# Turned hidden activations in a SwiGLU feed-forward: their splits later in the written order, their transfers on one queue, and four down columns in three passes

## The chip, the cores and the metric

The kernel runs on one core of a Trainium2 chip. A core has a matmul engine (PE, with its weight loads shown as PEld), a vector engine (DVE), a scalar engine (ACT), a general engine (POOL, or GpSimd) and a queue engine (SP). Each takes its own instructions in order; DMA transfers are issued from the queues of SP, ACT and POOL. The metric is the device time of one execution, in microseconds (us); lower is better.

## The reference, cut to what matters

Two layers of a decoder trunk on 256 tokens of width 1024, all in float32. Each layer is a feed-forward, a token mixer, a cross-attention to a memory of 256 rows, and a second feed-forward:

```python
def swiglu(x, w_gate, w_up, w_down):
    return (jax.nn.silu(x @ w_gate) * (x @ w_up)) @ w_down

for l in range(DEPTH):                       # DEPTH = 2, D_MODEL = 1024, D_FF = 2816
    x = x + 0.5 * swiglu(rmsnorm(x, ffn1_norm[l]), ffn1_w_gate[l], ffn1_w_up[l], ffn1_w_down[l])
    h = rmsnorm(x, mix_norm[l])
    x = x + (even_mixer(h, ...) if l % 2 == 0 else odd_mixer(h, ...))
    x = x + memory_cross_attention(rmsnorm(x, xa_norm[l]), mem_n, ...)
    x = x + 0.5 * swiglu(rmsnorm(x, ffn2_norm[l]), ffn2_w_gate[l], ffn2_w_up[l], ffn2_w_down[l])
return rmsnorm(x, final_norm)
```

The four feed-forwards, in order of time: ffn1 of layer 0 (called the first here), ffn2 of layer 0 (the second), ffn1 of layer 1 (the third) and ffn2 of layer 1 (the last, after which only the final norm follows).

## The kernel before, in words

**Numbers in two halves.** Every float32 operand of a matmul is split into a high part (a copy rounded to fp32r) and a low part (the rest), and a product is made of three: high by high, high by low, low by high. A split is one ACT copy and one DVE subtraction. Weights are split so on the chip, in blocks of eight 128x128 tiles: lines 127 (ACT, `whi`) and 128 (DVE, `wlo`). There are five buffers of such blocks, and `Stream.take` asks for the block that is needed and four more ahead. The raw weights come from HBM in the order in which the program takes them, 16 tiles to a transfer, on SP's queue (line 102).

**The order of the work.** `Order.run` writes the program in an order of its own: it has a list of fillers (pieces of matmul work, each with a test that says from when it is ready, the piece, and its cost) and a heap of tasks that are due some time after something else (`pe.after(delay, fn, cost)`). Its clock advances by the costs, which are in ns of matmul time. A task is run between two fillers, at the first point at which it is due. The instructions written so are then put in order on each engine by a scheduler with a simulated timeline, which may let an instruction go ahead of an earlier one that it takes to be not ready. `tc.keep_in_program_order` pins an instruction behind the one written just before it on its engine.

**A feed-forward.** The hidden width of 2816 is 22 tiles of 128 (`FT`). `hidden(f0)` makes four of them: eight pieces of 2600 in the order's time, first the gate (line 554 applies silu, on ACT) and then the up product (line 558 multiplies, on DVE). The last two tiles, f0=20, have gate and up side by side in one group of four pieces (lines 565 and 566). In the first feed-forward the scale of the norm is known only after the first group. These matmuls (lines 533 to 535) keep the activations in place and stream 512 weight columns, so the result has tokens on partitions.

**The turn.** The down product needs h with its own index on partitions. `turned_back` does that: DVE transposes within 32x32 blocks (line 507) into a tile `t` (named v or k2 in turn, one buffer each; v and k in the profile), one DMA writes it to a DRAM tile named turn (line 510), and four DMAs read it back with the blocks moved (line 512). Groups of four tiles use POOL's queue, the last group of two uses ACT's. Then each of the tiles is split: ACT copy in line 518, DVE subtraction in line 519. These are written directly after the transfers.

**The down columns.** `downs` makes the eight output tiles j, each a sum over 22 tiles k of h (lines 393 and 394; the last column uses a narrower form, line 398 to 400). Columns 0 and 1 first take k = 0 to 19, then both take k = 20 and 21; the others take all 22 in one go. A column's sum is in an `acc` bank; there are four `acc` banks, two `sc` (score) banks and two `tr` banks. At a column's end line 585 adds it to x in two steps on DVE, and lines 318 and 319 (ACT and DVE) make the next norm's operand, with squares for the norm's sum (lines 329, 333). The last feed-forward uses `down_tok` instead, which keeps tokens on partitions and takes two tiles of h at a time.

The next function bodies are those that the change touches, with the profile's line numbers.

Of the kernel before, what the change touches and what calls it, by code (L numbers as in the profile page):

```python
# [15 lines left out]
F32 = mybir.dt.float32  # L16
F32R = mybir.dt.float32r
AF = mybir.ActivationFunctionType
ALU = mybir.AluOpType
# [6 lines left out]
KT = D // P  # L26
S = 256
FF = 2816
FT = FF // P
# [189 lines left out]
def paired(t):  # L219

    return t.rearrange("p (b a) -> p a b", b=2)


def halves(t):

    return t.rearrange("p (b a) -> p b a", b=2)


def unpaired(ps):

    return ps.rearrange("p (a b) -> p b a", b=2)
# [12 lines left out]
def build(nc, tc, ctx, a):  # L244
# [6 lines left out]
    def acc_tile():  # L251
        return psum.tile([P, 512], F32, name="acc", bufs=4)
# [10 lines left out]
    def w2():  # L263
        return act.tile([P, 512], F32, name="w2", bufs=6)
# [5 lines left out]
    x = consts.tile([P, KT, S], F32, name="x")  # L270
# [22 lines left out]
    pe = Order()  # L293
# [176 lines left out]
    def h_tile():  # L470
        return Split(act.tile([P, 2 * S], F32R, name="h", bufs=FT))
# [26 lines left out]
    def ffn(which, layer, n, nxt, first=False, last=False):  # L498
        h = [None] * FT
        gate, up = f"{which}_w_gate", f"{which}_w_up"  # L500

        def turned_back(f0, s, c):

            t = act.tile([P, 8 * c * 32], F32, name=("v", "k2")[f0 // 4 % 2], bufs=1)
            to = t.rearrange("p (b u c i) -> p u c b i", b=4, u=2, c=c)
            for u in range(2):
                nc.vector.transpose(to[:, u], s[u].rearrange("p (c b j) -> p c b j", c=c, b=4))
            queue = nc.gpsimd if c == 4 else nc.scalar
            d = dram.tile([P, 8 * c * 32], F32, name="turn", bufs=2)
            queue.dma_start(d, t)  # L510
            for b in range(4):
                queue.dma_start(t[32 * b:32 * b + 32].rearrange("j (a x) -> j a x", a=4),
                                d.rearrange("(a j) (b x) -> b j a x", a=4, b=4)[b])
            back = t.rearrange("p (a u c i) -> p c u a i", a=4, u=2, c=c)
            for i in range(c):
                h[f0 + i] = x2 = h_tile()
                hi, lo = (m.rearrange("p u (a i) -> p u a i", a=4) for m in (x2.hi, x2.lo))
                nc.scalar.activation(hi, back[:, i], AF.Copy)
                nc.vector.tensor_tensor(lo, back[:, i], hi.bitcast(F32), op=ALU.subtract)  # L519

        def rows_of(name, c, bank, evac, other=None):

            ps = []

            def part(ks):
                def go():
                    if ks[0] == 0:
                        ps.extend(bank() for _ in range(2))
                    for k in ks:
                        wh, wl = (paired(w) for w in ws.take(name, layer, k * P, c, 4, other=other))  # L530
                        for u in range(2):
                            xh, xl = (n.x[k].v[:, u, m] for m in range(2))
                            nc.tensor.matmul(ps[u], xh, wh, start=k == 0, stop=False)  # L533
                            nc.tensor.matmul(ps[u], xh, wl, start=False, stop=False)  # L534
                            nc.tensor.matmul(ps[u], xl, wh, start=False, stop=k == KT - 1)  # L535
                    ws.flush()
                    if ks[-1] == KT - 1:
                        when_scaled(n, lambda: evac(ps))

                return always, go, len(ks) * 1300  # L540

            return [part(range(k, k + 2)) for k in range(0, KT, 2)]

        def hidden(f0):
# [24 lines left out]
            if f0 + 4 > FT:  # L569
                return rows_of(gate, f0 * P, acc_tile, both, up)  # L570
            return (rows_of(gate, f0 * P, sc_tile if f0 // 4 % 2 else acc_tile, gated) +
                    rows_of(up, f0 * P, acc_tile, product))

        def down(j, ks, cell):
            def go():
                if ks[0] == 0:
                    cell.append(acc_tile())
                ps = cell[0]
                ws.fine = j == KT - 1
                for k in ks:  # L580
                    w = ws.take(f"{which}_w_down", layer, k * P, j * P)
                    (mm_narrow if ws.fine else mm)(ps, w, h[k], k == 0, k == FT - 1)
                if ks[-1] == FT - 1:
                    for part in (ps[:, :S],) if ws.fine else (ps[:, :S], ps[:, S:]):
                        nc.vector.scalar_tensor_tensor(halves(x[:, j]), unpaired(part), 0.5, halves(x[:, j]),
                                                       op0=ALU.mult, op1=ALU.add)
                    normed_tile(nxt, j, x[:, j], x)
                ws.flush()

            return always, go, len(ks) * 327  # L590

        def downs():

            cells = [[] for _ in range(KT)]
            early = range(FT // 4 * 4)
            late = range(FT // 4 * 4, FT)
            return ([down(j, early, cells[j]) for j in range(2)] + [down(j, late, cells[j]) for j in range(2)] +
                    [down(j, range(FT), cells[j]) for j in range(2, KT)])

        def down_tok():  # L600

            late = 2 * (ws.BUFS - 1)
            pss, got, mean = {}, {}, [EPS, EPS]

            def part(fs, *regions):

                c = regions[0][1] // 512

                def go():
                    for f in fs:
                        if (f, c) not in got:
                            got[f, c] = ws.take(f"{which}_w_down", layer, f * P, c * 512, 4)
                        for reg in regions:
                            u, c0, c1 = reg
                            if f == 0:
                                pss[reg] = (sc_tile if c == 1 and c1 - c0 == 512 else acc_tile)()[:, :c1 - c0]
                            ps = pss[reg]
                            wh, wl = (paired(w)[:, (c0 - c * 512) // 2:(c1 - c * 512) // 2] for w in got[f, c])  # L620
                            hh, hl = (h[f].v[:, u, m] for m in range(2))
                            nc.tensor.matmul(ps, hh, wh, start=f == 0, stop=False)
                            nc.tensor.matmul(ps, hh, wl, start=False, stop=False)  # L623
                            nc.tensor.matmul(ps, hl, wh, start=False, stop=f == FT - 1)  # L624
                    if fs[-1] == FT - 1:
                        for u, c0, c1 in regions:
                            evac_tok(u, slice(c0, c1), pss[u, c0, c1])

                return always, go, sum(len(fs) * (c1 - c0) * 654 // 512 for _, c0, c1 in regions)

            def evac_tok(u, at, ps):
                y = xtok[:, u, at]
                nc.vector.scalar_tensor_tensor(y, ps, 0.5, y, op0=ALU.mult, op1=ALU.add)
                ms = act.tile([P, 1], F32, name="mean", bufs=4)
                junk = w2()[:, :at.stop - at.start]
                nc.vector.tensor_tensor_reduce(junk, y, y, 1.0 / D, mean[u], ALU.mult, ALU.add, ms)
                mean[u] = ms
                if at.stop < D:
                    nc.gpsimd.tensor_tensor(y, y, gfin[:, at], op=ALU.mult)
                    return  # L640
                r = act.tile([P, 1], F32, name="rcol", bufs=2)
                nc.gpsimd.tensor_tensor(r, ms, mhalf[:, 0:1], op=ALU.pow)
                nc.vector.tensor_tensor(y, y, gfin[:, at], op=ALU.mult)
                out = a["out"][u * P:(u + 1) * P]
                cuts = (0, 384, 704, D)
                nc.scalar.activation(xtok[:, u, :cuts[1]], xtok[:, u, :cuts[1]], AF.Copy, scale=r)
                nc.scalar.dma_start(out[:, :cuts[1]], xtok[:, u, :cuts[1]])
                for i, j in zip(cuts[1:], cuts[2:]):
                    nc.vector.tensor_scalar(xtok[:, u, i:j], xtok[:, u, i:j], r, None, op0=ALU.mult)
                    nc.sync.dma_start(out[:, i:j], xtok[:, u, i:j])  # L650

            end = range(FT - late, FT)
            right = ((0, 512, D), (1, 512, 768), (1, 768, D))
            return [part(range(i, i + 2), (0, 0, 512), (1, 0, 512)) for i in range(0, FT, 2)] + [
                part(range(FT - late), *right)] + [part(end, reg) for reg in right]

        if first:
# [469 lines left out]
    for k in range(KT):  # L1127
# [3 lines left out]
        cuts = (0, 1, SIDE) if k == 0 else (0, SIDE)  # L1131
# [9 lines left out]
    early = {}  # L1141
# [115 lines left out]
```

## Time and profile before

| what | value |
|---|---|
| three timed runs | 972.92, 975.81 (median), 977.94 us |
| the profiled execution, whole | 979.09 us |
| its span, first to last instruction | 977.3 us |
| PE busy in the span | 957.3 us (98%) |
| ACT, DVE, POOL busy | 556.4, 683.2, 106.8 us |
| mean granted clock of PE | 0.992 |

A row of the order of time has its start, its length, the engine, the line and operation, output<-input, how many were merged, and in brackets how long the engine stood idle before it and what ended that. A queue of an engine (ACTq, POOLq) shows what it issues. A row of the groups has the busy time, the mean of one in ns, and the idle time before the group with what ended most of it. A row of the waits has the total in us, the number, and the longest.

### The profile page before, as it was taken

The page shows a single profiled execution, that of the slowest core. Times are in us where ns is not written, and L with a number is a line of the kernel's source. Part 1 is how long each engine was busy: PE and PEld are TensorE (multiplying, and loading weights), DVE is VectorE, ACT ScalarE, POOL GpSimd, SP SyncE. Part 2 cuts the span into 40 slices and gives each one's busy share as a digit, 9 for nine tenths or more (in the row PEclk, how much of TensorE's full clock was granted, in tenths as well). Part 3 has the DMA queues.
Part 4 walks back from the last instruction along what each step waited for, and adds up shares of the span by engine and source line. Part 5 has one row for each costly group of instructions (what it writes and reads, how often), then busy time and mean ns, then how long its engine had stood idle before and what let it go on. Part 6 is the DMA issues. An engine that isn't in the chain of part 4 may idle for free.

```text
span 977.3 us, 15067 instructions
## 1 busy us (share of the span) xinstructions
PE 957.3 (98%) x5830; PEld 877.2 (90%) x5830; DVE 683.2 (70%) x1077; ACT 556.4 (57%) x903; POOL 106.8 (11%) x195
## 2 busy tenths in 40 slices
PE   9999969999999999999999999999999999999997
PEld 7888859999999988888998888999999998888896
DVE  7666557698878866666666666677887697677663
ACT  7554535498657754554555554555796585465541
POOL 0421110001000011120001111000000005511110
PEclk9999979999999999999999999999999999999999
DMA  9898765654444687866557787765635248987831
GB/s 372 317 369 278 251 214 203 216 215 148 165 165 136 243 273 259 266 236 206 211 207 234 249 258 260 227 222 190 243 130 195 93 173 291 322 274 233 267 137 43
DMA packets 39511, 219.67 MB, mean 225 GB/s; under 512 B 5768, under 2 KB 8840, under 8 KB 16784
## 3 DMA queue, kind: packets, MB, share of 16 engines
q1 hardware_dynamic: 27072, 187.44, 54.4%
q0 software_dynamic: 8912, 28.35, 9.7%
q10 hardware_dynamic: 3456, 2.93, 1.0%
q8 instruction: 45, 0.74, 0.3%
q14 instruction: 26, 0.21, 0.1%
HBM read 205.04 MB, written 16.80 MB: 227 GB/s over the span
## 4 chain that ended last, share of the span: by engine, by line
PE 86%; DMA 8%; issue 2%; POOL 2%; ACT 1%; DVE 1%; POOLq 0%; SPq 0%; DVEq 0%; ACTq 0%
PE acc L533 10%; PE acc L534 10%; PE acc L535 10%; PE acc L393 10%; PE acc L398 7%; PE acc L400 7%; PE acc L399 7%; PE acc L394 5%; DMA v<-turn 3%; PE sc L535 2%; PE sc L534 2%; PE sc L533 2%; DMA turn<-k 2%; PE acc L623 1%; PE acc L624 1%
## 5 line engine op out<-in xcount | busy, mean ns | idle before, releaser
L128 DVE TENSOR_TENSOR wlo<-raw,whi 128x1024 fp32r<-128x1024 f32 (+2 forms) x377 | 426.0, 1139 | 197.0 <-ACT whi L127 194.7
L127 ACT ACTIVATE whi<-raw 128x1024 fp32r<-128x1024 f32 (+2 forms) x377 | 367.0, 984 | 287.9 <-PE acc L535 121.1
L534 PE MATMUL acc<-wlo,x 128*128 128x512 f32 x576 | 218.5, 379 | 0.8 <-DVE wlo L128 0.8
L535 PE MATMUL acc<-whi,x 128*128 128x512 f32 x576 | 218.1, 379 | 0.0
L533 PE MATMUL acc<-whi,x 128*128 128x512 f32 x576 | 215.5, 380 | 1.4 <-ACT whi L127 1.4
L393 PE MATMUL acc<-h,whi 128*128 128x512 f32 x462 | 156.0, 390 | 9.9 <-DVE h L519 9.9
L394 PE MATMUL acc<-h,wlo 128*128 128x256 f32 x462 | 127.5, 277 | 0.0
L533 PEld LDWEIGHTS acc<-whi,x 128*128 128x128 f32 x576 | 108.8, 189 | 17.1 <-ACT whi L127 1.9
L534 PEld LDWEIGHTS acc<-wlo,x 128*128 128x128 f32 x576 | 108.9, 189 | 16.6 <-DVE wlo L128 1.4
L535 PEld LDWEIGHTS acc<-whi,x 128*128 128x128 f32 x576 | 108.9, 189 | 15.3
L393 PEld LDWEIGHTS acc<-h,whi 128*128 128x128 f32 x462 | 89.2, 194 | 23.5 <-DVE h L519 10.5
L394 PEld LDWEIGHTS acc<-h,wlo 128*128 128x128 f32 x462 | 90.7, 196 | 0.2
L400 PE MATMUL acc<-h,wlo 128*128 128x256 f32 x322 | 87.7, 275 | 0.0
L399 PE MATMUL acc<-h,whi 128*128 128x256 f32 x322 | 87.7, 275 | 0.0
L398 PE MATMUL acc<-h,whi 128*128 128x256 f32 x322 | 86.5, 277 | 0.0
L400 PE MATMUL acc<-x,wlo 128*128 128x256 f32 x304 | 84.1, 278 | 0.0
L399 PE MATMUL acc<-x,whi 128*128 128x256 f32 x304 | 83.8, 277 | 0.0
L398 PE MATMUL acc<-x,whi 128*128 128x256 f32 x304 | 83.3, 278 | 0.0
L399 PEld LDWEIGHTS acc<-h,whi 128*128 128x128 f32 x322 | 61.7, 192 | 0.1
L400 PEld LDWEIGHTS acc<-h,wlo 128*128 128x128 f32 x322 | 61.7, 192 | 0.1
L398 PEld LDWEIGHTS acc<-h,whi 128*128 128x128 f32 x322 | 60.6, 192 | 0.4 <-DVE x L461 0.2
L399 PEld LDWEIGHTS acc<-x,whi 128*128 128x128 f32 x304 | 58.2, 192 | 0.2
(220 smaller groups left out, 1402.8 us busy)
## 6 DMA issues: line engine op xcount, KB each, us to landing
raw<-in_w SPq DMA_DIRECT2D x171, 1024.0 KB, 5.0
turn<-v POOLq DMA_DIRECT2D x12, 512.0 KB, 3.3
v<-turn POOLq DMA_DIRECT2D x48, 128.0 KB, 4.6
turn<-k POOLq DMA_DIRECT2D x8, 512.0 KB, 4.6
k<-turn POOLq DMA_DIRECT2D x32, 128.0 KB, 5.4
dists<-line POOLq DMA_DIRECT2D x2, 1536.0 KB, 14.2
raw<-in_memT SPq DMA_DIRECT2D x3, 1024.0 KB, 5.0
raw<-in_w SPq DMA_DIRECT2D x6, 384.0 KB, 6.0
```

The lines of the kernel that those rows point to most:

```text
L127: for ins in (self.nc.scalar.activation(hi[:, at], src, AF.Copy), self.nc.vector.tensor_tensor(lo[:, at], src, hi[:, at].bitcast(F32), op= ...
L128: self.nc.vector.tensor_tensor(lo[:, at], src, hi[:, at].bitcast(F32), op=ALU.subtract)):
L393: nc.tensor.matmul(ps, w[0], x2.both, start=start, stop=False)
L394: nc.tensor.matmul(ps[:, :S], w[1], x2.high, start=False, stop=stop)
L398: nc.tensor.matmul(ps[:, :S], w[0], x2.high, start=start, stop=False)
L399: nc.tensor.matmul(ps[:, :S], w[0], x2.low, start=False, stop=False)
L400: nc.tensor.matmul(ps[:, :S], w[1], x2.high, start=False, stop=stop)
L533: nc.tensor.matmul(ps[u], xh, wh, start=k == 0, stop=False)
L534: nc.tensor.matmul(ps[u], xh, wl, start=False, stop=False)
L535: nc.tensor.matmul(ps[u], xl, wh, start=False, stop=k == KT - 1)
L623: nc.tensor.matmul(ps, hh, wl, start=False, stop=False)
L624: nc.tensor.matmul(ps, hl, wh, start=False, stop=f == FT - 1)
```

## The change

The split of the turned tiles becomes a function `split` that the order puts in 22000 (ns of its time) after the transfers were written, and its instructions are pinned in program order. All transfers of the turn go to GpSimd's queue, the last group's too. The down columns 0 to 3 are made in three passes over k, 0 to 15, 16 to 19 and 20 to 21; columns 4 to 7 take all 22 at once, and columns 4 and 5 take their banks from `sc`. A filler of the down product now tests whether the tiles of h that it names have been written (`have`), where it was always ready.

```diff
-            queue = nc.gpsimd if c == 4 else nc.scalar
             d = dram.tile([P, 8 * c * 32], F32, name="turn", bufs=2)
-            queue.dma_start(d, t)
+            nc.gpsimd.dma_start(d, t)
             for b in range(4):
-                queue.dma_start(t[32 * b:32 * b + 32].rearrange("j (a x) -> j a x", a=4),
-                                d.rearrange("(a j) (b x) -> b j a x", a=4, b=4)[b])
+                nc.gpsimd.dma_start(t[32 * b:32 * b + 32].rearrange("j (a x) -> j a x", a=4),
+                                   d.rearrange("(a j) (b x) -> b j a x", a=4, b=4)[b])
             back = t.rearrange("p (a u c i) -> p c u a i", a=4, u=2, c=c)
-            for i in range(c):
-                h[f0 + i] = x2 = h_tile()
-                hi, lo = (m.rearrange("p u (a i) -> p u a i", a=4) for m in (x2.hi, x2.lo))
-                nc.scalar.activation(hi, back[:, i], AF.Copy)
-                nc.vector.tensor_tensor(lo, back[:, i], hi.bitcast(F32), op=ALU.subtract)
+
+            def split():
+                for i in range(c):
+                    h[f0 + i] = x2 = h_tile()
+                    hi, lo = (m.rearrange("p u (a i) -> p u a i", a=4) for m in (x2.hi, x2.lo))
+                    tc.keep_in_program_order(nc.scalar.activation(hi, back[:, i], AF.Copy))
+                    tc.keep_in_program_order(nc.vector.tensor_tensor(lo, back[:, i], hi.bitcast(F32), op=ALU.subtract))
+
+            pe.after(22000, split, 0)
...
+        def have(ks):
+            return lambda: math.inf if any(h[k] is None for k in ks) else 0.0
+
         def down(j, ks, cell):
             def go():
                 if ks[0] == 0:
-                    cell.append(acc_tile())
+                    cell.append((sc_tile if j in (4, 5) else acc_tile)())
...
-            return always, go, len(ks) * 327
+            return have(ks), go, len(ks) * 327
 
         def downs():
 
             cells = [[] for _ in range(KT)]
-            early = range(FT // 4 * 4)
-            late = range(FT // 4 * 4, FT)
-            return ([down(j, early, cells[j]) for j in range(2)] + [down(j, late, cells[j]) for j in range(2)] +
-                    [down(j, range(FT), cells[j]) for j in range(2, KT)])
+            cuts = (0, FT // 4 * 4 - 4, FT // 4 * 4, FT)
+            return ([down(j, range(*cut), cells[j]) for cut in zip(cuts, cuts[1:]) for j in range(4)] +
+                    [down(j, range(FT), cells[j]) for j in range(4, KT)])
...
-                return always, go, sum(len(fs) * (c1 - c0) * 654 // 512 for _, c0, c1 in regions)
+                return have(fs), go, sum(len(fs) * (c1 - c0) * 654 // 512 for _, c0, c1 in regions)
```

The second `have` is in `down_tok`.

## The prediction

> **What bounds the kernel now.** I read the page first, then the waits of the matmul engine, then the order of time around each wait, engine by engine.
>
> ```profile
> span 977.3 us, 15067 instructions
> PE 957.3 (98%) x5830; PEld 877.2 (90%) x5830; DVE 683.2 (70%) x1077; ACT 556.4 (57%) x903; POOL 106.8 (11%) x195
> PE   9999969999999999999999999999999999999997
> PEclk9999979999999999999999999999999999999999
> ```
>
> PE is busy for 957.3 of 977.3 us, so no change of order can win more than the 20.0 us of idle time plus whatever the busy time contains of slow matmuls. The sixth slice (122 to 147 us) is the only inner one with a hole, and the same slice has the low clock. The wait of PE for a turned h (total, times, longest):
>
> ```profile
> PE acc L393 <- DVE h L519: 9.9, 2, 8.1
> ```
>
> Both are of a down column (L393) for the split of a turned h (L519). In order of time on PE, with a third and short wait for a weight split:
>
> ```profile
> 117.38 0.48 PE L534 MATMUL acc<-wlo,x 128*128 128x512 f32 x1 [0.78 <-DVE wlo L128]
> 122.45 0.38 PE L393 MATMUL acc<-h,whi 128*128 128x512 f32 x1
> 139.23 0.79 PE L393 MATMUL acc<-h,whi 128*128 128x512 f32 x1 [8.11 <-DVE h L519]
> 145.11 0.38 PE L393 MATMUL acc<-h,whi 128*128 128x512 f32 x1
> ...
> 437.33 0.38 PE L393 MATMUL acc<-h,whi 128*128 128x512 f32 x1
> 437.66 0.38 PE L393 MATMUL acc<-h,whi 128*128 128x512 f32 x1
> 447.84 0.48 PE L393 MATMUL acc<-h,whi 128*128 128x512 f32 x1 [1.83 <-DVE h L519]
> 449.03 0.63 PE L393 MATMUL acc<-h,whi 128*128 128x512 f32 x1
> 452.23 0.40 PE L393 MATMUL acc<-h,whi 128*128 128x512 f32 x1
> ```
>
> That is 10.7 us of waits; the other 9.3 us of idle time are the start and the tail, which the change does not touch. After a wait the matmuls run slow. A window of 5 us inside the first such stretch (busy time of PE, PEld, DVE, ACT and POOL, then the granted clock, the DMA share and GB/s):
>
> ```profile
> 140.00:145.00 5.00, 5.00 (x18) 4.26 (x17) 3.34 (x6) 3.67 (x5) 0.00 (x0) 0.50 0.14 38
> ```
>
> From 139.23 to 145.11 (5.88 us) PE ran at clock 0.50, which costs 2.9 us; from 449.03 to 452.23 (3.2 us) again, 1.6 us. So a wait costs itself and a slow stretch: 8.11 + 2.9 and 1.83 + 1.6, and 0.78 with nothing behind it.
>
> *A rule against the row:* the Trainium skill (TensorE: Matmul & The Clock Gate, What's actually happening) lets the clock fall only after an idle window of about 3.4 us. Here 1.83 us of idle were followed by a half clock. By the rule a left-over wait below 3.4 us would cost itself alone; by the row it costs 1.6 us more, and the row is what I use.
>
> **Why h came late.** ACT, DVE and the queues in the first feed-forward:
>
> ```profile
> 113.79 1.34 ACT L518 ACTIVATE h<-k 128x256 fp32r<-128x256 f32 x4 [9.65 <-DMA k<-turn]
> 114.24 1.43 DVE L519 TENSOR_TENSOR h<-k,h 128x256 fp32r<-128x256 f32 x4 [8.84 <-ACT h L518]
> 118.46 1.40 DVE L558 SCALAR_TENSOR_TENSOR w<-acc,rcol,w 128x512 f32<-128x512 f32 x2
> 122.50 0.59 POOL L510 DMA_DIRECT2D turn<-v  x1 [16.43 <-DVE v L507]
> 126.34 2.20 POOL L512 DMA_DIRECT2D v<-turn  x4 [3.24 <-DMA turn<-v]
> 127.34 0.34 ACTq L510 DMA_DIRECT2D turn<-k  x1
> 138.31 0.42 ACT L518 ACTIVATE h<-v 128x256 fp32r<-128x256 f32 x1 [9.47 <-DMA v<-turn]
> 138.42 0.34 ACTq L512 DMA_DIRECT2D k<-turn  x1
> 142.95 0.71 ACT L518 ACTIVATE h<-k 128x256 fp32r<-128x256 f32 x2
> ```
>
> The reader should see a chain of two links. ACT stood 9.65 us at the split of f0=12 for its transfer; DVE, in order too, stood 8.84 us behind it and came to the product of f0=16 (L558) only at 118.46, so the write of f0=16 went out at 122.50. Its data came back at 138.31, 15.8 us later, and the down column, begun at 122.45, needed it after 16 of its steps. And f0=20's reads, on ACT's own queue, could not go out before 138.42, behind that same split.
>
> **The change, part by part.** Write T for the moment when the last row matmul of a group is in. One down step (row to row, 437.33 to 437.66) is 0.33 us; the order's cost for it is 327, so its units are ns. Group f0=20 is 8 k of 1300, 10.4 us: T16 = 122.45 - 10.4 = 112.0 and T12 = 91.2 in the first feed-forward; T16 = 426.9 and T20 = 437.3 in the second.
>
> *Splits 22000 later.* A group of four is 20.8 us, so the split is put in after the next group's product and one further row part: T + 22 to T + 23.4. For f0=12 that is 113, and its data came at 113.79: ACT stands about 1 us, not 9.65, and the product of f0=16 is now ahead of that split on DVE. That takes the 0.78 us wait and the first link. In the second feed-forward, with DVE not held, the write of f0=16 goes out at:
>
> ```profile
> 432.71 0.56 POOL L510 DMA_DIRECT2D turn<-v  x1 [14.45 <-DVE v L507]
> 439.24 0.34 ACTq L510 DMA_DIRECT2D turn<-k  x1
> 446.91 0.42 ACT L518 ACTIVATE h<-v 128x256 fp32r<-128x256 f32 x1 [5.75 <-DMA v<-turn]
> ...
> 615.00 0.34 ACTq L510 DMA_DIRECT2D turn<-k  x1
> 621.51 2.29 ACTq L512 DMA_DIRECT2D k<-turn  x4
> 627.51 0.72 ACT L518 ACTIVATE h<-k 128x256 fp32r<-128x256 f32 x2 [1.60 <-DMA k<-turn]
> ```
>
> that is T16 + 5.8, and its data is there by T16 + 20.0. The first feed-forward then issues at 117.8 and, at its own slower 15.8 us, has the data at 133.6, T16 + 21.6.
>
> *Four columns in three passes.* Pass 1 is 4 x 16 steps, 20.9 us; pass 2 needs f0=16 at T20 + 20.9 = T16 + 31.3; pass 3 needs f0=20 at T20 + 26.2. The split of f0=16 is put behind the third column of pass 1 (T16 + 26.1 in the order; its instructions reach ACT at about T16 + 24.5, as weight splits run four blocks ahead), that of f0=20 behind the first column of pass 2 (T20 + 22.2). Both are past the data and ahead of the need. The passes alone would do it: even at today's times h of f0=16 (139.2) is before 122.45 + 20.9 = 143.4 and that of f0=20 (about 145) before 148.6. So 8.11 + 2.9 and 1.83 + 1.6 go.
>
> *All transfers on GpSimd's queue.* Five issues per feed-forward move, in all four. On ACT they lay beside the matmuls and win nothing themselves. On POOL they stand behind f0=16's four reads (126.34 + 2.20), which are out before f0=20's write (127.34); then a wait for the write and four issues at 0.55 us. From write to last data took 12.5 us at 615.00 to 627.51 on ACT's queue. Bounds in the first feed-forward: 127.34 + 12.5 = 139.8, early by 7 us; or with the longest rows, 11.1 us (127.34 to 138.42) for the write and 12.0 us (126.34 to 138.31) for the reads, 150.4: with 1.2 us of splits, 3 us after 148.6, and 1.6 to 2.9 us of half clock. So 0 to 6 us; I take 0, since the long rows both contain ACT's stand.
>
> *Against the change* the Trainium skill (SBUF — State Buffer, section SBUF: two separate sides) says that a DMA issued from GpSimd can be held while DVE has the port they share. This view of one line (min/median/max ns) shows no such hold:
>
> ```profile
> L512 POOL DMA_DIRECT2D v<-turn x48: 553/553/581, 40.7 to 911.6; - x48
> ```
>
> The 48 issues lie beside DVE at 70% busy and none took over 581 ns. By the rule each of the five issues could be held for one weight split of 1.23 us, and the far bound above would be 12 us in place of 6; by the row it stays at 6, and so I leave it.
>
> *Banks and the end of the columns.* Columns 0 to 3 keep all four acc banks until pass 3, columns 4 and 5 take the two score banks, free since the gate of f0=12. Column 2 needs the bank of f0=20's rows at T20 + 10.5; these were read before the turn of 127.34, T20 + 4.9. In pass 3 four columns end within 2.6 us where two did:
>
> ```profile
> L128 DVE TENSOR_TENSOR wlo<-raw,whi 128x1024 fp32r<-128x1024 f32 x316 | 385.5, 1227 | 188.0 <-ACT whi L127 186.5
> L319 DVE SCALAR_TENSOR_TENSOR x<-x,vecs 128x256 fp32r<-128x256 f32 x56 | 26.1, 478 | 1.2 <-ACT x L318 1.2
> L585 DVE SCALAR_TENSOR_TENSOR x<-acc,x 128x256 f32<-128x256 f32 x45 | 18.7, 422 | 9.3 <-PE acc L394 6.5 <-PE acc L400 2.3
> ```
>
> DVE gets 4 x (2 x 0.422 + 0.478) = 5.3 us at once. The weight splits' lead, four blocks of 8 steps or 10.5 us, hides it; without that lead it would be 5.3 us in each of three feed-forwards. Matmuls, weight bytes and vector work are the same in number. The test for a missing h acts in the order's time alone and puts no wait on the chip.
>
> *The pins.* Behind a split that stands on ACT queue the weight splits, and behind these PE. The place to watch is f0=4 of the first feed-forward, whose data comes latest after its group:
>
> ```profile
> 68.96 1.06 ACT L127 ACTIVATE whi<-raw 128x1024 fp32r<-128x1024 f32 x1 [1.53 <-PE acc L535]
> 82.96 1.33 ACT L518 ACTIVATE h<-k 128x256 fp32r<-128x256 f32 x4 [7.70 <-DMA k<-turn]
> ```
>
> Today ACT stands 7.70 us there and PE loses nothing. The split now may follow at 70.0 at the earliest (T4, two groups before T12, is 49.6, and T4 + 20.8 is 70.4): 12.9 us of standing, against five blocks of 2.6 us that end at 81.9 while the next weight split is ready at 82.96 + 1.33 + 1.06 + 1.23 = 86.6: 4.7 us of wait and 1.6 to 2.9 us of half clock, 7 us. So 0 to 7; I take 0, because the scheduler let weight splits pass while it thought the data not landed, and it still may.
>
> **Sum.** 8.11 + 2.9 + 1.83 + 1.6 + 0.78 = 15.3 us less, nothing added: 979.09 (the profiled execution) - 15.3 = 963.8. The median shown is 975.81, 3.3 us below the profiled one, the runs 972.92 to 977.94. If that difference is a shorter wait in those runs, they come to 963.8 as well; if it is common to all, to 960.5. I say 962.
>
> **Rivals.** (A) One wait is left in the first feed-forward, f0=4 at its early place or f0=20 landing late: 6 to 7 us back, 969. For it: f0=4's data came 33 us after T4 (82.96 against 49.6), f0=12's 22.6 us after T12; against it: both need the far end of a bound. Chance 0.20. (B) No difference, 974: the waits only move on, DVE's 5.3 us of pass 3 adding to a late f0=20 in each of three feed-forwards, some 4 to 5 us apiece. Against it stands the 10.5 us lead. Chance 0.07. (C) Slower: the pins hold ACT both at f0=4 (7 us) and, before its lead is rebuilt, at f0=8, whose data comes late too (ACT stood there until 96.56):
>
> ```profile
> 86.60 4.84 ACT L127 ACTIVATE whi<-raw 128x1024 fp32r<-128x1024 f32 x5
> 96.56 1.34 ACT L518 ACTIVATE h<-v 128x256 fp32r<-128x256 f32 x4 [5.12 <-DMA v<-turn]
> ```
>
> If the lead were gone, that is 5.1 of standing, 1.3 of split, 2.3 of the next weight split and 2.9 of slow clock, 11.6, and with 7 it passes the 15.3 gained: 979. It decides only if PE finds no block ready at 91.4; ACT made five between 86.60 and 91.44 in the run shown, one in 1.0 us against 2.6 us that PE takes for it. Chance 0.04. (D) The change doesn't do what it says, since the scheduler reorders: then the passes still move the need 15 us back, so this is not a separate time.
>
> **How the numbers follow.** Forecast 0.66 (958 to 966.5), A 0.20, B 0.07, C 0.04, and 0.03 for more than forecast. A measurement of this kernel tells some 0.5%, 4.9 us, from no change: faster is below 970.9. That holds for the forecast, the excess and most of A (0.86); same is B and a little of A (0.10); slower is C (0.04). The range goes from 957 to 971, into A; the forecast's own is 958 to 966.5.
>
> **What would show it.** Right: no wait of L393 for L519; granted clock 1.00 from 120 to 150 and at 450; PE busy falling by about 4.5 us as the slow matmuls go; ACT standing 1 us or less at f0=12's split; the write of f0=16 issued near 118. Wrong: a wait of PE for whi or wlo between 80 and 100 (A or C), a wait in pass 3 for h of f0=20 (A), or waits for wlo just after pass 3 (B). A time near 975 with these waits gone would mean that matmuls got slower, and the step on equal matmuls would be wrong.

## The result, and the profile after

The changed kernel takes 966.5 us (median of five runs, 963.3 to 968.64), the kernel before 975.81 (five runs, 972.92 to 977.94); the ratio is 0.990, 95% interval 0.9869 to 0.993. Faster was forecast, at 962.0 with a range of 957 to 971. The gain is 9.3 us where 13.8 were forecast.

The profiled execution took 966.5 us, its span is 964.7, 12.6 us shorter than before. From its page: the span, the busy times, PE in 40 slices, and the granted clock.

```profile
span 964.7 us, 15082 instructions
PE 954.2 (99%) x5830; PEld 875.5 (91%) x5830; DVE 681.0 (71%) x1077; ACT 557.3 (58%) x903; POOL 118.0 (12%) x215
PE   9999999999999999999999999999999999999996
PEclk9999999999999999999999999999999999999998
```

The hole in the sixth slice is gone, in busy time and in clock. The waits of PE that are left, beside 0.8 us ahead of its first instruction (total, times, longest), answer to the row of 9.9 us before:

```profile
PE acc L536 <- ACT whi L127: 0.9, 1, 0.9
PE tr L367 <- POOL rcolm L361: 0.6, 1, 0.6
```

The first is at the start of the program. The second, at 108.62, is new: the scale of the memory norm, which POOL computes behind four reads of a turned group. In order of time, the splits of h on ACT in the first feed-forward (line 519 now), f0=4 to f0=20; the bracket is how long ACT stood before them:

```profile
84.65 1.33 ACT L519 ACTIVATE h<-k 128x256 fp32r<-128x256 f32 x4 [7.74 <-DMA k<-turn]
99.30 1.33 ACT L519 ACTIVATE h<-v 128x256 fp32r<-128x256 f32 x4 [6.18 <-DMA v<-turn]
116.35 1.34 ACT L519 ACTIVATE h<-k 128x256 fp32r<-128x256 f32 x4 [1.67 <-DMA k<-turn]
...
137.94 1.32 ACT L519 ACTIVATE h<-v 128x256 fp32r<-128x256 f32 x4
...
145.79 0.71 ACT L519 ACTIVATE h<-k 128x256 fp32r<-128x256 f32 x2
```

At f0=12 the stand fell from 9.65 to 1.67 us; at f0=16 and f0=20 there is none. The transfers of f0=16 and f0=20 on POOL:

```profile
117.31 0.59 POOL L509 DMA_DIRECT2D turn<-v  x1 [8.75 <-DVE h L520]
121.84 2.19 POOL L511 DMA_DIRECT2D v<-turn  x4 [3.93 <-DMA turn<-v]
125.95 0.56 POOL L509 DMA_DIRECT2D turn<-k  x1 [1.92 <-DVE k L507]
131.41 2.17 POOL L511 DMA_DIRECT2D k<-turn  x4 [4.89 <-DMA turn<-k]
```

The write of f0=16 goes out at 117.31 instead of 122.50; f0=20's reads are out by 133.6 instead of after 138.42. What this execution still loses is at its start, on PE:

```profile
5.40 1.22 PE L536 MATMUL acc<-whi,x 128*128 128x512 f32 x2 [0.87 <-ACT whi L127]
6.42 0.63 PE L537 MATMUL acc<-wlo,x 128*128 128x512 f32 x1
...
10.24 0.38 PE L538 MATMUL acc<-whi,x 128*128 128x512 f32 x1
```

A matmul takes 0.63 us until 10.24 and 0.38 from there on. Half speed for 4.8 us costs 2.4 us. It is read from the length of the matmuls: the column of the granted clock says 1.00 from 5 to 10 us. That start is a matter of the execution and not of the change: another execution of the same kernel began with matmuls of 0.38 us, and one of the kernel before with 0.63.

### The profile page after: what moved, and what is told of

Same layout as the page of the kernel before. It is cut to its first block, busy times and chain, and to the rows that moved or that the text cites. A ratio compares the mean times of both kernels' runs of the same rounds, so it can differ in the third digit from the quotient of the medians.

```text
span 964.7 us, 15082 instructions
## 1 busy us (share of the span) xinstructions
PE 954.2 (99%) x5830; PEld 875.5 (91%) x5830; DVE 681.0 (71%) x1077; ACT 557.3 (58%) x903; POOL 118.0 (12%) x215
## 4 chain that ended last, share of the span: by engine, by line
PE 90%; DMA 5%; POOL 1%; issue 1%; DVE 1%; ACT 0%; POOLq 0%; SPq 0%; DVEq 0%; ACTq 0%
PE acc L536 11%; PE acc L537 11%; PE acc L538 11%; PE acc L393 7%; PE acc L398 7%; PE acc L400 7%; PE acc L399 7%; PE acc L394 4%; PE sc L393 3%; DMA turn<-k 3%; PE sc L538 2%; PE sc L536 2%; PE sc L537 2%; PE acc L629 1%; PE acc L628 1%; PE sc L394 1%
## 5 line engine op out<-in xcount | busy, mean ns | idle before, releaser
L538 PEld LDWEIGHTS acc<-whi,x 128*128 128x128 f32 x576 | 109.5, 190 | 15.6
L537 PEld LDWEIGHTS acc<-wlo,x 128*128 128x128 f32 x576 | 109.5, 190 | 15.6
L393 PE MATMUL acc<-h,whi 128*128 128x512 f32 x330 | 108.5, 382 | 0.0
L394 PE MATMUL acc<-h,wlo 128*128 128x256 f32 x330 | 90.0, 273 | 0.0
L400 PE MATMUL acc<-h,wlo 128*128 128x256 f32 x322 | 87.7, 275 | 0.0
L393 PEld LDWEIGHTS acc<-h,whi 128*128 128x128 f32 x330 | 62.4, 189 | 8.6
L394 PEld LDWEIGHTS acc<-h,wlo 128*128 128x128 f32 x330 | 63.3, 192 | 0.2
L399 PEld LDWEIGHTS acc<-h,whi 128*128 128x128 f32 x322 | 61.7, 192 | 0.1
L400 PEld LDWEIGHTS acc<-h,wlo 128*128 128x128 f32 x322 | 61.7, 192 | 0.1
L398 PEld LDWEIGHTS acc<-h,whi 128*128 128x128 f32 x322 | 60.6, 192 | 0.4 <-DVE x L461 0.2
```

The lines of the kernel that those rows point to most:

```text
L393: nc.tensor.matmul(ps, w[0], x2.both, start=start, stop=False)
L394: nc.tensor.matmul(ps[:, :S], w[1], x2.high, start=False, stop=stop)
L398: nc.tensor.matmul(ps[:, :S], w[0], x2.high, start=start, stop=False)
L399: nc.tensor.matmul(ps[:, :S], w[0], x2.low, start=False, stop=False)
L400: nc.tensor.matmul(ps[:, :S], w[1], x2.high, start=False, stop=stop)
```

## The experiments

All were timed in five rounds beside the kernel before, which had medians of 976.16 (first four rows), 976.24 (next four), 977.57 (next three) and 974.55 us.

| run | edit | median us (range) | ratio, 95% interval |
|---|---|---|---|
| before_again | none, kernel before | 973.35 (970.38–979.81) | 0.9976, 0.9951–1.0001 |
| passes | three passes and score banks alone | 970.42 (964.21–973.91) | 0.9926, 0.9897–0.9954 |
| late | late pinned splits alone | 965.86 (963.63–971.75) | 0.9893, 0.9862–0.9925 |
| after_again | none, changed kernel | 965.56 (963.46–966.2) | 0.9879, 0.9855–0.9902 |
| nopin | changed kernel without the pins | 970.6 (966.18–974.22) | 0.9945, 0.9924–0.9966 |
| actq | last group on ACT's queue again | 964.91 (962.75–968.55) | 0.9885, 0.9864–0.9907 |
| accbanks | columns 4 and 5 in acc banks | 971.85 (968.32–975.93) | 0.9954, 0.9932–0.9976 |
| warm | three more warm-up matmuls | 966.25 (965.48–967.23) | 0.9896, 0.9879–0.9914 |
| delay14 | splits 14000 later, not 22000 | 969.98 (966.9–973.31) | 0.9926, 0.99–0.9953 |
| spread | memory norm's scale used later | 964.77 (963.5–971.04) | 0.9881, 0.9846–0.9916 |
| warm_spread | warm and spread together | 969.18 (963.82–971.12) | 0.9908, 0.9872–0.9943 |
| bias_later | warm, spread, bias tables late | 965.71 (965.51–966.45) | 0.9905, 0.9886–0.9925 |

### Which part makes the gain

The prediction had said that the passes alone would remove both waits. The two parts were run apart, beside both kernels unchanged.

> The kernel before, unchanged, so that a second profiled execution stands beside the first. Its first profiled execution took 979.09 us with 9.9 us of PE waits for a turned h, while its runs had a median of 975.81. If the waits themselves differ from execution to execution, this profile shows another total (between 3 and 12 us), and its time follows that total and the speed of PE at the start. If the waits are fixed and the difference lies elsewhere, it shows 9.9 us again to within 1 us. Time in the runs: 975.8, within 2 us.

> The kernel before with the three passes and the two score banks alone; splits stay where they were written, the last group's transfers stay on ACT's queue. Theory 1 (the passes alone move the need past the data): no PE wait for a turned h, ACT still stands at the split of f0=12 in the first feed-forward (about 9 us) and a PE wait of up to 1 us behind it may stay; 966 to 968 us, the same as the full change within 1.5 us. Theory 2 (the late splits are what counts, since they free DVE for the product of f0=16): waits of several us stay and the time is 971 or more.

```diff
-                    cell.append(acc_tile())
+                    cell.append((sc_tile if j in (4, 5) else acc_tile)())
...
-            early = range(FT // 4 * 4)
...
+            cuts = (0, FT // 4 * 4 - 4, FT // 4 * 4, FT)
+            return ([down(j, range(*cut), cells[j]) for cut in zip(cuts, cuts[1:]) for j in range(4)] +
+                    [down(j, range(FT), cells[j]) for j in range(4, KT)])
```

> The kernel before with the late, pinned splits alone; two columns as before (20 tiles, then 2), the last group's transfers on ACT's queue. Theory 1: PE still needs f0=16 some 5.2 us after the last group, 15.6 us after its own product's matmuls, and its data takes 20 us or more from there, so PE waits 3 to 5 us in the first and 1 to 3 us in the second feed-forward, each with a slow stretch behind it; 969 to 973 us. Theory 2: the waits are gone or under 1 us, and the time is that of the full change, 966 to 967.

```diff
+            def split():
...
+                    tc.keep_in_program_order(nc.scalar.activation(hi, back[:, i], AF.Copy))
...
+            pe.after(22000, split, 0)
```

> The changed kernel, unchanged, for a second profile on the same chip as the other three. Its first profile had PE at half clock from 5.4 to 10.2 us, where the kernel before had full clock from its first real matmul. If that is chance in each execution, it may be gone here and the time be some 2.4 us lower; if it belongs to the changed kernel, it is there again. Time in the runs: 966.5, within 2 us; no PE wait for a turned h.

In the second execution of the kernel before, the same wait is shorter:

```profile
PE acc L393 <- DVE h L519: 5.7, 1, 5.7
```

5.7 us in place of 9.9, and its span is 971.6 in place of 977.3. So the size of the wait differs between executions, and the 9.9 of the profile that the prediction worked from is the longer of the two seen.

With the passes alone, the wait of PE for h is gone, and another stands in its place:

```profile
PE acc L393 <- ACT whi L127: 3.0, 1, 3.0
PE acc L394 <- DVE wlo L128: 0.8, 1, 0.8
```

PE now waits for a weight split. ACT and PE of the same run, in order of time, show why:

```profile
114.33 1.33 ACT L518 ACTIVATE h<-k 128x256 fp32r<-128x256 f32 x4 [8.64 <-DMA k<-turn]
...
128.33 1.06 ACT L127 ACTIVATE whi<-raw 128x1024 fp32r<-128x1024 f32 x1 [3.71 <-PE acc L393]
138.77 0.42 ACT L518 ACTIVATE h<-v 128x256 fp32r<-128x256 f32 x1 [9.38 <-DMA v<-turn]
...
140.77 2.00 ACT L127 ACTIVATE whi<-raw 128x1024 fp32r<-128x1024 f32 x2 [0.67 <-ACT h L518]
...
141.88 0.48 PE L393 MATMUL acc<-h,whi 128*128 128x512 f32 x1 [3.01 <-ACT whi L127]
```

ACT stood 9.38 us at the split of f0=16 and split no weights meanwhile. One weight split ended at 129.39 and the next began at 140.77, 11.4 us later, and PE's lead of four blocks, 10.5 us, ran out. A slow stretch follows: the granted clock was 0.80 from 140 to 145 us. The passes took away PE's need for h, but ACT met the split of h as early as before. The quickest of these runs took 964.21 us, which would fit a stand shorter than the lead; no profile of such a run was taken.

The late splits alone give what the whole change gives, 965.86 against 965.56 us, and the passes alone 970.42. In its profile one wait for h is left:

```profile
136.10 0.48 PE L393 MATMUL acc<-h,whi 128*128 128x512 f32 x1 [1.88 <-DVE h L521]
```

It is not a wait for the data of f0=16, whose reads went out from 120.88 on and landed in a median of 6.9 us. ACT came late to the split: in this run the reads of f0=20 are on its own queue, ahead of that split, and they waited for a write that took 8.0 us. (For such a stand the row names "issue" and no releaser.)

```profile
132.63 2.36 ACTq L512 DMA_DIRECT2D k<-turn  x4
135.17 1.33 ACT L520 ACTIVATE h<-v 128x256 fp32r<-128x256 f32 x4 [8.75 <-issue]
```

So the passes, and with them the move to GpSimd's queue, are at most a reserve against this 1.9 us, which the medians don't show. Late splits with the move and without the passes were not run.

### The pins and the delay

> The changed kernel without the two pins; the split is still written 22000 later. Its order on ACT has the split of f0=12 (first feed-forward) three weight splits earlier than the changed kernel and that of f0=16 four earlier, so the scheduler puts them about where they were. If what counts is where ACT meets a split whose data is not there (new theory, after the passes-alone run), ACT stands some 9 us at f0=12 and f0=16 again, PE waits 2 to 4 us for a weight split and runs a slow stretch: 968 to 971 us, like the passes alone. If writing the split later is enough by itself, 965 to 967.

```diff
-                    tc.keep_in_program_order(nc.scalar.activation(hi, back[:, i], AF.Copy))
-                    tc.keep_in_program_order(nc.vector.tensor_tensor(lo, back[:, i], hi.bitcast(F32), op=ALU.subtract))
+                    nc.scalar.activation(hi, back[:, i], AF.Copy)
+                    nc.vector.tensor_tensor(lo, back[:, i], hi.bitcast(F32), op=ALU.subtract)
```

Without pins 5.0 us of the gain are lost (970.6 against 965.56; the intervals of the ratios do not meet). ACT stands at f0=12 and f0=16 of the first feed-forward as in the kernel before:

```profile
113.58 1.34 ACT L519 ACTIVATE h<-k 128x256 fp32r<-128x256 f32 x4 [9.40 <-DMA k<-turn]
...
136.27 1.34 ACT L519 ACTIVATE h<-v 128x256 fp32r<-128x256 f32 x4 [10.26 <-DMA v<-turn]
```

What ended ACT's idle time ahead of line 519, in the four feed-forwards together (us, times), without the pins:

```profile
  DMA k<-turn: 31.2, 9
  DMA v<-turn: 27.5, 8
```

and in the changed kernel:

```profile
  DMA k<-turn: 9.7, 3
  DMA v<-turn: 6.2, 1
```

58.7 us of standing against 15.9. On ACT the split of f0=12 comes behind 47 weight splits and that of f0=16 behind 55, just as in the kernel before; in the changed kernel it is 50 and 59. So without a pin the scheduler moves the split up again, and on top of the passes the delay alone gains nothing (970.6 against 970.42 for the passes); the pin holds it. How the stands cost the 5 us is shown in part only: the profiled execution, 966.75 us, is one of the two quickest of eight, and in it PE waits 2.1 us for weight splits with no slow stretch. That the longer ones lose more in the same places is argued.

> The changed kernel with 14000 in place of 22000; pins, passes, banks and queue as changed. If what counts is where ACT meets a split whose data is not there, its stands at f0=12 and f0=16 of the first feed-forward come back (5 to 9 us each), the write of f0=16 goes out near 122 in place of 117, PE waits 1 to 3 us for weight splits and runs slow stretches in some executions: 968 to 971 us, between the changed kernel (966) and the one before, near the passes alone (970.4) and the one without pins (970.6). If the passes had made the place of the splits free, 965 to 967.

```diff
-            pe.after(22000, split, 0)
+            pe.after(14000, split, 0)
```

Eight microseconds earlier cost 4.4 us (969.98 against 965.56; the intervals of the ratios just touch). ACT stands everywhere again, f0=4, f0=12 and f0=16, and PE waits after the first of them:

```profile
87.34 1.34 ACT L519 ACTIVATE h<-k 128x256 fp32r<-128x256 f32 x4 [9.76 <-DMA k<-turn]
...
89.98 0.48 PE L536 MATMUL acc<-whi,x 128*128 128x512 f32 x1 [1.08 <-ACT whi L127]
...
91.24 0.48 PE L537 MATMUL acc<-wlo,x 128*128 128x512 f32 x1 [0.78 <-DVE wlo L128]
...
116.19 1.34 ACT L519 ACTIVATE h<-k 128x256 fp32r<-128x256 f32 x4 [6.13 <-DMA k<-turn]
...
138.86 1.34 ACT L519 ACTIVATE h<-v 128x256 fp32r<-128x256 f32 x4 [7.94 <-DMA v<-turn]
```

Behind the two waits of PE the granted clock was 0.72 from 90 to 95 us. The stands at f0=12 and f0=16 came back as expected, but PE lost nothing behind them in this execution.

### The queue and the banks

> The changed kernel with the last group's five transfers back on ACT's queue. The prediction gave the move nothing: 965.6 within 2 us, no PE wait for h; ACT then stands some 5 to 8 us at its own wait for the write of f0=20, which the lead of 10.5 us in weight splits covers. Rival: that stand costs as the others did, with a PE wait for a weight split of 1 us or more in one of the feed-forwards, 967 to 970.

```diff
+            queue = nc.gpsimd if c == 4 else nc.scalar
...
-            nc.gpsimd.dma_start(d, t)
+            queue.dma_start(d, t)
```

964.91 us, no inner wait: once the passes are there, the queue of the last group is worth nothing that can be measured.

> The changed kernel with columns 4 and 5 in the acc banks like the others. Column 4 then needs column 0's bank 2 us after column 0's last matmul, when DVE has just got the ends of four columns (5.3 us of work, column 0's two adds of 0.42 first). Expected: a PE wait under 1 us in each of three feed-forwards, if any, and 965.6 to 968. Rival: DVE comes to column 0 only behind a weight split and PE waits 2 us or more in each, with slow stretches: 970 or more.

```diff
-                    cell.append((sc_tile if j in (4, 5) else acc_tile)())
+                    cell.append(acc_tile())
```

971.85 us, 6.3 more than the changed kernel. The waits of PE, then one of the three in order of time:

```profile
PE acc L393 <- DVE x L591: 4.3, 3, 1.4
```

```profile
151.35 0.45 PE L393 MATMUL acc<-h,whi 128*128 128x512 f32 x1 [1.42 <-DVE x L591]
```

In pass 3 four columns end close together, and column 4 waits for DVE to empty a bank (line 591), 1.4 us in three feed-forwards. The profiled execution, 968.64 us, is one of the two quickest of eight; its span of 966.9 is 5.2 above that of the second profile of the changed kernel (961.7), and the 4.3 us are most of that. No slow stretch follows in it (granted clock 1.00 from 151 to 156 us). The median lies 3.2 us higher still: the slowest of the timed runs, 975.93 and 975.21 us, had a mean clock of 0.995 and 0.996 against 0.998 here, which would fit slow stretches behind some of these waits. That is argued from the clock alone. The passes therefore need the score banks: with late splits and no passes, the same banks as before give 965.86; with passes and no score banks, 971.85.

### What is left: the start and f0=4

> The changed kernel with 11 in place of 8 of the matmuls on zeros with which PE starts. In five of the six profiles so far PE stood 0.9 to 1.4 us between these and its first real matmul, and in four of the six it then ran some 4 us at half speed, which costs 2.4 us. If the gap brings that about, the matmuls start at full speed in the profile and the median falls by 1 to 2.4 us against the changed kernel, to 963 to 965; if it is chance apart from the gap, the median stays at 965.6.

```diff
-WARM = 8
+WARM = 11
```

With three more warm-up matmuls PE runs at full speed from its first real matmul in the profile, and the time is the same, 966.25. In that profile a wait for the memory norm's scale stands against what the start gained:

```profile
PE tr L367 <- POOL rcolm L361: 2.4, 1, 2.4
```

> The changed kernel with the memory norm's scale taken 15000 (in place of 2200) after its sums. PE waited 0.6 us for that scale in the first profile of the changed kernel and 2.4 us in the run with 11 matmuls on zeros, since GpSimd makes it only behind the reads of f0=12, which wait for their write. Expected: that wait gone, 0 to 2 us less than the changed kernel, 964 to 966.

```diff
-            pe.after(*((2200, spread, 120) if wide else (1400, known, 0)))
+            pe.after(*((15000 if n.keep else 2200, spread, 120) if wide else (1400, known, 0)))
```

> Both, 11 matmuls on zeros and the later scale. If the 11 matmuls gained 2.4 us at the start and lost it again at the wait for the memory norm's scale (which does not come earlier when PE does), both together give what each alone does not: full clock from the start, no inner PE wait, 962 to 964 us. If the start's clock is not worth what it seems, 965 to 966.

With that scale used later, the wait is gone and the median is 964.77, no different from the changed kernel. Both edits together gave 969.18, against the expectation; its interval overlaps those of the two alone, so that it is slower is not shown. ACT and PE at f0=4 in that run, and its clock behind it (window, busy PE, PEld, DVE, ACT, POOL, granted clock, DMA share, GB/s):

```profile
86.82 1.33 ACT L519 ACTIVATE h<-k 128x256 fp32r<-128x256 f32 x4 [11.88 <-DMA k<-turn]
...
89.46 0.48 PE L536 MATMUL acc<-whi,x 128*128 128x512 f32 x1 [2.67 <-ACT whi L127]
...
90.72 0.79 PE L537 MATMUL acc<-wlo,x 128*128 128x512 f32 x1 [0.78 <-DVE wlo L128]
```

```profile
90.00:95.00 5.00, 4.28 (x12) 3.53 (x13) 4.13 (x5) 4.34 (x5) 0.72 (x2) 0.66 0.97 315
```

This is rival A's mechanism: a stand of 11.88 us is longer than the lead, PE waits 2.67 and 0.78 us, and a slow stretch follows. The earlier start of PE is not what makes the stand so long. ACT came to this split at 74.9 us, as in the run with the warm-up alone (74.9) and in the second profile of the changed kernel (74.7). There the data was in at 82.4 and 80.0 and PE lost nothing; here it was in at 86.8. The changed kernel's own stands, 7.74 and 5.26 us in its two profiles, were short of the lead.

> The changed kernel with three edits: the bias tables of the first mixer are made behind the first finished down column (about 149 us) instead of at 30 us, so that their writes and the read of the bias no longer stand between the turn's transfers of f0=0, f0=4 and f0=8 on GpSimd's queue; the spread of the memory norm's scale is put in 15000 instead of 2200 after it; three more warm-up matmuls. Theory (the stand of ACT at f0=4 is set by transfers, in which the write of f0=4, issued at 54.1, took 18.6 us to land beside the 3 MB of the tables): the write lands in some 8 us or less, the data of f0=4 is there before its split comes at about 77, ACT stands under 1 us there and at most 2 us at f0=8, so no inner wait of PE is left in any execution; full clock from the first matmul; median 961 to 963, with the runs closer together than 3 us. Rival 1 (the turn's time is set by the weight stream and not by the tables): the stand at f0=4 stays at 6 to 12 us and the median at 964 to 969. Rival 2 (the tables now come too late): the first softmax, at about 200 us, or the scale of the mixer's norm behind the read of the bias on GpSimd, at about 181 us, makes PE wait 2 us or more; median 966 or more.

```diff
-        make_bias(n.rcol)
+        make_bias(x[:, 0])
...
-    pe.after(30000, biases, 0)
+    pe.after(148000, biases, 0)
```

This run also has the edits of warm and spread, so warm_spread is the run that differs from it by the tables alone. POOL around f0=4's transfers in the changed kernel, then in this one:

```profile
51.65 1.09 POOL L914 DMA_DIRECT2D dists<-line  x2 [6.44 <-DMA line<-kT]
...
54.09 0.56 POOL L509 DMA_DIRECT2D turn<-k  x1
63.01 0.92 POOL L921 DMA_DIRECT2D bias<-dists  x1 [8.36 <-DMA dists<-line]
72.67 2.22 POOL L511 DMA_DIRECT2D k<-turn  x4 [8.73 <-DMA turn<-k]
```

```profile
52.41 0.56 POOL L509 DMA_DIRECT2D turn<-k  x1 [9.83 <-DVE k L507]
56.51 2.18 POOL L511 DMA_DIRECT2D k<-turn  x4 [3.54 <-DMA turn<-k]
```

The reads of f0=4 went out 18.6 us after its write where the bias tables' transfers (3 MB of writes, 1 MB read) lie beside them, and 4.1 us after it without them. The write itself took 18.3 us to land in the first case and 3.8 us in the second. In warm_spread, too, the reads went out 18.6 us after the write, and the write took 18.3. ACT's split now finds its data:

```profile
72.77 1.32 ACT L519 ACTIVATE h<-k 128x256 fp32r<-128x256 f32 x4
...
92.75 1.34 ACT L519 ACTIVATE h<-v 128x256 fp32r<-128x256 f32 x4 [1.54 <-DMA v<-turn]
```

The cause of f0=4's stand is thus shown: 11.88 us in warm_spread, none here. Rival 1 of this run falls; so does rival 2, since PE has no wait at the first softmax or the mixer's norm. The forecast of 961 to 963 us falls too: 965.71. The six runs lie within 0.94 us, where the two sets of the changed kernel spread over 5.3 and 2.7. PE has one new inner wait, in the mixer:

```profile
250.74 0.71 PE L398 MATMUL acc<-h,whi 128*128 128x256 f32 x4 [0.96 <-ACT h L466]
```

With one of 0.20 just behind it that is 1.2 us, and its span of 964.4 is 2.7 longer than that of the second profile of the changed kernel (961.7). The first softmax came at 201.9 us, where it came at 199.9 in the changed kernel's profile, though PE was 2.1 us ahead at 148. PE has no wait in between, no row names what held the softmax back, and the other 1.5 us stay open. No version beat the changed kernel by a measurable amount.

## Why the prediction was right, and where its size was off

**What bounds the kernel:** right. Only the waits of the first and second feed-forward and the slow stretches behind them could be won, and they are gone. One reading is off: PE stood for h of f0=16 from 131.1 on (139.23 less 8.11), which is 26 steps behind the start of the down column at 122.45 and not 16. The sum does not use it.

**Splits 22000 later:** right, and the step that carries the gain. Forecast: ACT stands about 1 us at f0=12 (1.67), the product of f0=16 is ahead of the split (it starts at 113.27, not 118.46), the write goes out at 117.8 (117.31). The prediction booked only 0.78 us and "the first link" to it.

```profile
113.27 1.40 DVE L561 SCALAR_TENSOR_TENSOR w<-acc,rcol,w 128x512 f32<-128x512 f32 x2
```

**"The passes alone would do it":** wrong; this step failed. It compared the time at which h is there with the time at which PE needs it, and forgot that ACT, standing for h, splits no weights. The passes alone left 3.8 us of waits for weight splits and a slow stretch in the profiled execution and came to 970.42. The sum came out near because the other part does it; for this step that is luck.

**All transfers on GpSimd's queue, worth 0:** right beside the passes (actq). Of the bounds, 139.8 to 150.4 for f0=20's data, the near one held: the reads are out by 133.6, landed in a median of 5.1 us, and the split at 145.79 didn't stand.

**Banks:** the text gave columns 4 and 5 the score banks without a price. They are worth 6.3 us once there are passes. The 5.3 us of DVE work in pass 3 were seen and the lead of weight splits covers them, but a bank that is not yet empty is a different wait, which that lead doesn't cover.

**The pins, 0 to 7 us of cost, taken at 0:** the profiled execution bears the 0 out (7.74 us of standing at f0=4, 7.70 before). The far end is real in kind, as warm_spread shows (2.67 and 0.78 us of wait and a slow stretch). But the sign was missed: the pins are worth 5 us, and rival D, the scheduler moving the splits back, was set aside because "the passes still move the need 15 us back". Run without pins, it is a time of its own, 970.6.

**The sum:** 15.3 us were taken from an execution of 979.09. The prediction left open whether the 3.3 us between that one and the median were a shorter wait; the second profile of before, with 5.7 us of waits for 9.9, speaks for that. Then the end is 963.8, and executions of 963.3 and 963.46 us were measured. The medians, 966.5 and 965.56, lie 2 to 3 us above it, and 3.6 to 4.5 above the 962 that was forecast. In the profiled one it is the slow start (2.4 us) and the wait for the memory norm's scale (0.6): 15.3 less 3.0 is 12.3, against 12.6 measured between the spans. The second profile of the changed kernel had neither: PE is busy for 951.8 us in it instead of 954.2, and its span of 961.7 is 15.6 us below the first of the kernel before. So the terms are right in size for these executions, and what the sum left out is what an execution loses at its start and at that scale. In others it may also be f0=4, which no profile of the changed kernel itself has caught.

**The rivals:** A did not come in the medians. Its mechanism was seen in warm_spread and delay14; whether it makes the slower executions of the changed kernel, up to 968.64 us, is not shown. B and C did not come, and D's claim of no separate time fell. B's kind of wait, DVE in pass 3, does come when the score banks are taken away.

## What to carry to other kernels

Ask of an operation that waits for a transfer not only who needs its result, but what its engine would do meanwhile: an engine that works in order and stands longer than the lead of its other products stops whoever lives on these. Put such an operation where its data is surely there, and hold it there if something reorders the program. When the consumer is moved back instead, price each resource that it holds longer, and look for the stand that will be met next.

## What the runs showed of the hardware that was not expected

A gap on PE does not decide by its length alone whether matmuls slow down after it. 1.83 us (before) was followed by matmuls at half speed for 3.2 us. 2.36 us (warm, until 108.36), 1.88 us (late) and 1.42 us (accbanks) were not followed by any. Two gaps close together were: 2.67 and 0.78 us (warm_spread, granted clock 0.66) and even 1.08 and 0.78 us (delay14, 0.72). The rows of late for the 5 us from the gap on and of warm from 110 on (its clock was 1.00 from 105 to 110 too), with the same columns as above:

```profile
136.00:141.00 5.00, 4.90 (x29) 4.50 (x30) 4.56 (x8) 4.91 (x8) 0.00 (x0) 1.00 0.10 20
```

```profile
110.00:115.00 5.00, 5.00 (x25) 4.38 (x24) 3.13 (x5) 2.37 (x3) 0.00 (x0) 1.00 0.94 257
```

The Trainium skill (TensorE: Matmul & The Clock Gate, What's actually happening) describes an activity window of about 3.4 us that runs freely, so that its place against the work differs from run to run. That part fits 1.83 and 2.36 us ending differently, and the start of the program being slow in some executions only. Its figure of one idle window of 3.4 us does not agree: a single gap of 1.83 us was enough.
